# Three instead of two chunk pairs a stage as seven block products, and two of the four weight sums made by adding DMA loads

## Chip, cores and metric

The kernel runs on one core of a Trainium2 chip. The metric is device time in microseconds (us) of one execution; the kernel before has a median of 1264.96 us over 3 runs (1264.08 to 1266.33).

## What is computed

Two layers; each has two feed-forward stages (FFN) with a mixer between them, all in float32 on 256 rows of 1024. Cut to the part that the change touches:

```
def swiglu(h, wi, wo):
    gate, up = jnp.split(h @ wi, 2, axis=-1)
    return (jax.nn.silu(gate) * up) @ wo
...
    for l in range(DEPTH):
        h = rms_norm(x, ffn1_pre_g[l])
        x = x + 0.5 * rms_norm(swiglu(h, ffn1_wi[l], ffn1_wo[l]), ffn1_post_g[l])
        h = rms_norm(x, mix_pre_g[l])
        ...
        h = rms_norm(x, ffn2_pre_g[l])
        x = x + 0.5 * rms_norm(swiglu(h, ffn2_wi[l], ffn2_wo[l]), ffn2_post_g[l])
```

So there are four FFN stages. The first product, `h @ wi`, has 1024 x 5632 weights, the second 2816 x 1024.

## The kernel before

**Tiling.** The 256 rows are two token tiles of 128 (`tt`). The 2816 hidden columns are 11 chunks of 256 gate and 256 up columns, so a chunk of the first product is one 128x512 accumulator per token tile. A unit is 1 MB of weights (128 partitions x 2048); a chunk's first product takes two units (`u11`, `u21` for its lower and upper 512 contraction rows), its second product one. To reach float32 accuracy every weight is split into two parts: ScalarE rounds half a unit to `hi` (line 217), VectorE computes the residue `lo` (line 218), and TensorE makes three matmuls of 512 columns (`mm3`, lines 383 to 385). TensorE takes `hi` and `lo` from a ring of 8 half units, which is 4 units: a slot is free again when TensorE has used it.

**Chunk pairs.** Two neighbouring chunks, two token tiles and two halves of the contraction make 8 block products of 12 matmuls each. For the pairs that begin at a chunk in `QUADS`, `pair7` makes them from 7 products by a Strassen-like scheme. Its weight operands are seven units, in the order of the plan: `B11` (u11), `T2`, `B21` (u21), `T3`, `T1`, `T4`, `B22` (u22), with two units `w` of the second product between them: B11, T2, w, B21, T3, T1, w, T4 (its weights are sum `f`), B22. Four of the operands are sums: T1 = u11 + u12, T2 = u11 + u12 + u22, T3 = u12 + u22, T4 = T2's sum + u21. They are made in tiles `a` (u11, later T1; `wa` in the profile), `b` (u12, later T3; `wb`) and `f` (T2, later T4; `wf`).

**Order of the work.** A planner with estimated times (`Clock`) writes every engine's instruction list at build time; on the chip each engine works through its list in order. The generator `loader` issues the loads on SP's queue, a few items ahead of `splitter`, which issues `hi`, `lo` and the sums. Plain units stream through two buffers of 1 MB (`raw`). Loads of `a` and `b` for one pair wait until T1 of the pair before has been split, since `a` still holds its weights.

**Accumulators of the first product** rotate through two buffers (`pmm`, tag "mm"). A pair takes four in turn: b0, b1, then a third for T1's product, to which B22's is added, and a fourth for T4. What frees the third is a subtraction on VectorE (`post`, line 536) that starts once B22's product is complete:

```
            b0 = mm()
            prod(b0, *s1, take(1)[0], True)
            chunk(j + 1, 1, b0, u3, ALU.subtract)
            wo2(j - 1)
            b1 = mm()
            prod(b1, *A(1, 4), take(1)[0], True)
            chunk(j, 1, b1, u3, ALU.add)
            prod(b0, *s4, take(1)[0], False)
            chunk(j + 1, 0, b0, u2, ALU.subtract)
```

In the kernel before, the pair at chunk 4 and the pair at chunk 8 each are followed by two units of the second product, which use other accumulators; chunks 6 and 7 are plain.

Of the kernel before, what the change touches and what calls it, by code (L numbers as in the profile page):

```python
# [13 lines left out]
ALU = mybir.AluOpType  # L14
# [10 lines left out]
EPS = 1e-6  # L25
NEG = -1.0e30
UNITS = 106
QUADS = (4, 8)

NOSYNC = mybir.DependencyInfo(mybir.DependencyClass.NoSync, mybir.DependencyReason.DATA)  # L30
HOT = 60
# [4 lines left out]
def f32(ap):  # L36
    return ap.bitcast(F32)
# [40 lines left out]
def trunk(ctx, tc, x, wpk, gains, lnp, wst, bst, consts, out, depth=DEPTH):  # L78
    nc = tc.nc
    V, S, G, T = nc.vector, nc.scalar, nc.gpsimd, nc.tensor  # L80
# [11 lines left out]
    def nm(s):  # L92
        cnt[0] += 1
        return f"{s}_{cnt[0]}"
# [18 lines left out]
    def load(dst, src):  # L113

        i = nc.sync.dma_start(dst, src)
        if lastdma[0] is not None:
            tc.add_manual_dep(i.ins, lastdma[0].ins.name, NOSYNC, reason="load order")
        lastdma[0] = i
# [9 lines left out]
    for l in range(depth):  # L128
        for st0, qj in ((0, QUADS), (33, None), (73, QUADS)):
            b = UNITS * l + st0  # L130
# [4 lines left out]
            def c(j, q):  # L135
                return b + (2 * j if j < 2 else 3 * j - 1 if j < NCH - 1 else 28) + q
# [5 lines left out]
            for j in range(2, NCH - 1, 2):  # L142
                if j in qj:
                    k = Quad({}, c(j, 0), c(j, 1), c(j + 1, 0), c(j + 1, 1))
# [12 lines left out]
    WQ = (slice(0, 1024), slice(1024, 2048))  # L157
    done, raw = set(), {}

    def loader():  # L160

        ring = []

        def stream(key, u, first=False):
            while len(ring) >= 2 and ring[-2] not in done:
                yield
            ring.append(key)
            t = rp.tile([P, 2048], F32, tag="raw", name=f"raw{u}", bufs=2)
            raw[key] = [t[:, c] for c in WQ]
            for c in WQ if first else (slice(0, 2048),):  # L170
                load(t[:, c], wpk[u][:, c])

        for n, (kind, k) in enumerate(plan):
            if kind == "w":
                yield from stream(n, k, n == 0)
            elif kind == "B11":
                while k.prev and not k.prev.t1:
                    yield
                f = k.ffn
                if not f:  # L180
                    for t in "ab":
                        f[t] = [sp.tile([P, 1024], F32, tag="q4", name=nm("w" + t), bufs=9) for _ in WQ]
                raw[n] = f["a"]
                for t, u in ((f["a"], k.u11), (f["b"], k.u12)):
                    for q, c in enumerate(WQ):
                        load(t[q], wpk[u][:, c])
                yield from stream(k, k.u22)
            elif kind in ("B21", "B22"):
                yield from stream(n, k.u21 if kind == "B21" else k.u22)
            yield  # L190

    ld = loader()

    def ready(n, kind, k):
        if kind[0] == "T":
            raw[n] = k.ffn[{"T1": "a", "T2": "f", "T3": "b", "T4": "f"}[kind]]
        return n in raw and (kind != "B11" or k in raw)

    def splitter():
        for n, (kind, k) in enumerate(plan):  # L200
            while not ready(n, kind, k):
                next(ld)
            halves[n] = []
            for q in range(2):
                gate = place.get(n)
                while st_["free"] <= 0 if gate is None else not gate.on:
                    yield 0.2
                    gate = place.get(n)
                if gate is not None:
                    h = sp.tile([P, 1024], F32R, tag="q4", name=f"hi{n}_{q}", bufs=9)  # L210
                    lo = sp.tile([P, 1024], F32R, tag="q4", name=f"lo{n}_{q}", bufs=9)
                else:
                    st_["free"] -= 1
                    h = rp.tile([P, 1024], F32R, tag="hi", name=f"hi{n}_{q}", bufs=RING)
                    lo = rp.tile([P, 1024], F32R, tag="lo", name=f"lo{n}_{q}", bufs=RING)
                r = raw[n][q]
                S.copy(h, r)  # L217
                V.tensor_sub(lo, r, f32(h))  # L218
                halves[n].append((h, lo))
                yield 1.2  # L220
            if kind == "B11":
                f = k.ffn
                if "f" not in f:
                    f["f"] = [sp.tile([P, 1024], F32, tag="xn", name=nm("wf"), bufs=2) for _ in WQ]
                for q in range(2):
                    V.tensor_add(f["a"][q], f["a"][q], f["b"][q])
                    V.tensor_add(f["f"][q], f["a"][q], raw[k][q])
                    yield 1.2
            elif kind == "T2":
                for q in range(2):  # L230
                    V.tensor_add(k.ffn["b"][q], k.ffn["b"][q], raw[k][q])
                    yield 0.6
                done.add(k)
            elif kind == "B21":
                for q in range(2):
                    V.tensor_add(k.ffn["f"][q], k.ffn["f"][q], raw[n][q])
                    yield 0.6
            elif kind == "T1":
                k.t1 = True
            done.add(n)  # L240
            for _ in range(3):
                next(ld, None)
# [27 lines left out]
    def gain(i):  # L270
        if i not in gl and i < 6 * depth:
            t = sp.tile([P, DM], F32, tag="gain", name=f"gain{i}", bufs=2)
            load(t, gains[i:i + 1, :].broadcast_to([P, DM]))
            gl[i] = t
        return gl.get(i)
# [149 lines left out]
    def ffn(gi, nxt, first):  # L425
# [3 lines left out]
        always.on = True  # L429
        for i in (32 + 3 * len(QUADS), 33 + 3 * len(QUADS)):  # L430
            place[st_["pos"] + i] = always
# [143 lines left out]
        for j in range(2, NCH - 1):  # L575
            if j == 4:
# [3 lines left out]
                gain(gi + 2)  # L580
            if j // 2 * 2 in QUADS:
                if j % 2 == 0:
# [333 lines left out]


    ck.start(splitter(), 7.0)
    for tt in range(NT):
        hready[tt] = Flag()  # L920
# [5 lines left out]
    for l in range(depth):  # L926
        b = 6 * l
# [102 lines left out]
```

## Time and profile before

| | us |
|---|---|
| median of 3 runs | 1264.96 |
| the profiled execution, its own time | 1265.89 |
| its span, first to last instruction | 1263.5 |
| TensorE busy in the span | 1248.7 (99%) |
| VectorE busy | 930.6 (74%) |
| ScalarE busy | 701.8 (56%) |
| GpSimd (POOL) busy | 34.6 (3%) |

Matmuls overlap, so a busy TensorE is to be read with the distance from one matmul's start to the next. The DMA engines moved 242.62 MB. About 0.2% (2.5 us) is what a measurement of this kernel can tell from no change.

### The profile page before, as it was taken

The numbers are of one execution on the slowest core, as the hardware profiler recorded it, in microseconds if no ns is written. First come the engines' busy times: TensorE is split into PE (matmuls) and PEld (weight loads), VectorE is DVE, ScalarE is ACT, GpSimd is POOL, SyncE is SP. The second block draws the span as 40 slices with busy tenths as digits, with TensorE's granted clock in tenths as the row PEclk, the third lists the DMA queues.
The fourth block names the chain that finished last, engine by engine and source line by source line (L and its number), as shares of the span: only waits on it lengthen the run. The fifth ranks groups of instructions, "written<-read, shape, count | busy, mean of one in ns | idle before, by whom it ended". The sixth has DMA issues, their size and how long they took to land.

```text
span 1263.5 us, 16239 instructions
## 1 busy us (share of the span) xinstructions
PE 1248.7 (99%) x6332; PEld 1040.4 (82%) x6332; DVE 930.6 (74%) x1157; ACT 701.8 (56%) x968; POOL 34.6 (3%) x81
## 2 busy tenths in 40 slices
PE   8999999999999999999999999999999999999997
PEld 7788888998778888888888888789977788888886
DVE  5897977646765979878768878765466568798783
ACT  6565665445666555656655646644366655556462
POOL 0000001000000010000000000010000000000000
PEclk9999999999999999999999999999999999999999
DMA  7757465555335545675645665654544355465651
GB/s 250 267 196 294 141 235 178 195 182 192 112 131 200 199 167 200 215 252 170 215 175 197 213 252 192 220 190 163 204 168 134 134 197 200 143 227 208 223 189 63
DMA packets 38381, 242.62 MB, mean 192 GB/s; under 512 B 4512, under 2 KB 4640, under 8 KB 12320
## 3 DMA queue, kind: packets, MB, share of 16 engines
q1 hardware_dynamic: 38304, 241.59, 54.1%
q8 instruction: 49, 0.80, 0.2%
q14 instruction: 28, 0.23, 0.1%
HBM read 240.52 MB, written 1.05 MB: 191 GB/s over the span
## 4 chain that ended last, share of the span: by engine, by line
PE 91%; DVE 4%; DMA 2%; ACT 2%; issue 1%; POOL 0%; SPq 0%; DVEq 0%; POOLq 0%; ACTq 0%
PE mm L383 16%; PE mm L385 16%; PE mm L384 16%; PE acc L385 6%; PE acc L384 6%; PE acc L383 6%; PE qk L384 3%; PE qk L383 3%; PE qk L385 3%; PE tr L330 3%; DMA raw<-wpk 2%; DVE lo L218 2%; PE pj L385 1%; PE pj L383 1%; PE pj L384 1%; ACT hi L217 1%
## 5 line engine op out<-in xcount | busy, mean ns | idle before, releaser
L218 DVE TENSOR_TENSOR lo<-raw,hi 128x1024 fp32r<-128x1024 f32 x392 | 470.2, 1221 | 166.2 <-ACT hi L217 160.8
L217 ACT CAST hi<-raw 128x1024 fp32r<-128x1024 f32 x392 | 402.9, 1049 | 266.2 <-DMA raw<-wpk 72.4
L383 PE MATMUL mm<-hi,hh 128*128 128x512 f32 x864 | 344.8, 399 | 1.1 <-ACT hh L323 1.1
L385 PE MATMUL mm<-hi,hl 128*128 128x512 f32 x864 | 338.4, 392 | 0.2 <-DVE hl L324 0.2
L384 PE MATMUL mm<-lo,hh 128*128 128x512 f32 x864 | 338.3, 392 | 0.0
L383 PEld LDWEIGHTS mm<-hi,hh 128*128 128x128 f32 x864 | 162.8, 188 | 36.0 <-issue 2.7
L385 PEld LDWEIGHTS mm<-hi,hl 128*128 128x128 f32 x864 | 162.6, 188 | 35.5 <-DVE hl L324 0.9
L384 PEld LDWEIGHTS mm<-lo,hh 128*128 128x128 f32 x864 | 163.1, 189 | 30.9
L383 PE MATMUL acc<-hi,gT 128*128 128x512 f32 x352 | 140.5, 399 | 0.0
L385 PE MATMUL acc<-hi,gT 128*128 128x512 f32 x352 | 138.0, 392 | 0.0
L384 PE MATMUL acc<-lo,gT 128*128 128x512 f32 x352 | 137.5, 390 | 0.0
L383 PE MATMUL qk<-hh,hi 128*128 128x256 f32 x320 | 91.3, 285 | 0.0
L385 PE MATMUL qk<-hh,lo 128*128 128x256 f32 x320 | 90.7, 284 | 0.0
L384 PE MATMUL qk<-hl,hi 128*128 128x256 f32 x320 | 90.7, 284 | 0.0
L385 PEld LDWEIGHTS acc<-hi,gT 128*128 128x128 f32 x352 | 66.1, 188 | 13.9
L384 PEld LDWEIGHTS acc<-lo,gT 128*128 128x128 f32 x352 | 66.3, 188 | 12.7
L383 PEld LDWEIGHTS acc<-hi,gT 128*128 128x128 f32 x352 | 66.2, 188 | 12.7 <-ACT gT L323 0.2
L323 ACT CAST gT<-tr 128x256 fp32r<-128x256 f32 x88 | 32.5, 369 | 73.8 <-PE tr L330 73.6
L384 PEld LDWEIGHTS qk<-hl,hi 128*128 128x128 f32 x320 | 61.5, 192 | 0.1
L383 PEld LDWEIGHTS qk<-hh,hi 128*128 128x128 f32 x320 | 61.5, 192 | 0.1
L385 PEld LDWEIGHTS qk<-hh,lo 128*128 128x128 f32 x320 | 61.5, 192 | 0.0
L324 DVE TENSOR_TENSOR gT<-tr,gT 128x256 fp32r<-128x256 f32 x88 | 36.8, 419 | 20.8 <-ACT gT L323 20.1
(170 smaller groups left out, 1552.3 us busy)
## 6 DMA issues: line engine op xcount, KB each, us to landing
raw<-wpk SPq DMA_DIRECT2D x203, 1024.0 KB, 4.9
wa<-wpk SPq DMA_DIRECT2D x16, 512.0 KB, 7.0
wb<-wpk SPq DMA_DIRECT2D x16, 512.0 KB, 8.9
gain<-gains SPq DMA_DIRECT2D x12, 512.0 KB, 7.1
x<-x SPq DMA_DIRECT2D x2, 512.0 KB, 5.6
raw<-wpk SPq DMA_DIRECT2D x2, 512.0 KB, 6.5
ln<-lnp SPq DMA_DIRECT2D x4, 256.0 KB, 5.7
out<-x SPq DMA_DIRECT2D x4, 256.0 KB, 2.0
```

The source lines that it names most:

```text
L217: S.copy(h, r)
L218: V.tensor_sub(lo, r, f32(h))
L323: lasthi[0] = S.copy(h_out, src)
L324: V.tensor_sub(l_out, src, f32(h_out))
L330: T.transpose(tr[:, k * P:(k + 1) * P], src[:, k * P:(k + 1) * P], ident)
L383: T.matmul(o, ah, bh, start=first, stop=False, skip_group_check=go_on)
L384: T.matmul(o, ah, bl, start=False, stop=False, skip_group_check=go_on)
L385: T.matmul(o, al, bh, start=False, stop=stop, skip_group_check=go_on)
```

## The change

Chunks 6 and 7 become a pair as well, so that a stage has three pairs in a row (chunks 4 to 9). In all pairs, two sums move from VectorE to DMA: T3 = b + u22 and T1 = a + u12 are made by DMA loads issued from GpSimd's queue that add what they read to what lies in the tile. The loads of u22 and u12 for this come to 2 MB a pair; before, u22 was loaded once for it into a `raw` buffer, and u12 was not loaded a second time. T2's sum is now f = a + b, after b has become u12 + u22, and before a becomes u11 + u12.

```
-QUADS = (4, 8)
+QUADS = (4, 6, 8)
...
                 for t, u in ((f["a"], k.u11), (f["b"], k.u12)):
                     for q, c in enumerate(WQ):
                         load(t[q], wpk[u][:, c])
-                yield from stream(k, k.u22)
+                for q, c in enumerate(WQ):
+                    nc.gpsimd.dma_start(f["b"][q], wpk[k.u22][:, c], accum_op=ALU.add)
...
-        return n in raw and (kind != "B11" or k in raw)
+        return n in raw
...
-                for q in range(2):
-                    V.tensor_add(f["a"][q], f["a"][q], f["b"][q])
-                    V.tensor_add(f["f"][q], f["a"][q], raw[k][q])
-                    yield 1.2
-            elif kind == "T2":
-                for q in range(2):
-                    V.tensor_add(k.ffn["b"][q], k.ffn["b"][q], raw[k][q])
+                for q, c in enumerate(WQ):
+                    V.tensor_add(f["f"][q], f["a"][q], f["b"][q])
+                    nc.gpsimd.dma_start(f["a"][q], wpk[k.u12][:, c], accum_op=ALU.add)
                     yield 0.6
-                done.add(k)
```

How it moves instructions, at three places of the second FFN stage of layer 0. TensorE's list of the kernel before, where the pair at chunk 4 ends (`mm_4535` is its third accumulator, B22's product the last written to it; `acc` are accumulators of the second product):

```order
L385 MATMUL mm_4535<-hi_1_4544,sA_4217 128x512
L383 MATMUL acc_4111<-hi_0_4556,gT_4511 128x512 [waits Activation_49]
L384 MATMUL acc_4111<-lo_0_4557,gT_4511 128x512
L385 MATMUL acc_4111<-hi_0_4556,gT_4511 128x512
L330 MATMUL tr_4661<-ident,cc_4630 128x128 [waits DVE_49,PE_49]
```

The same place in the changed kernel (`mm_4562` is the third accumulator, `mm_4686` the next pair's first, and of the same buffer):

```order
L381 MATMUL mm_4562<-hi_1_4571,sA_4242 128x512
L379 MATMUL mm_4686<-hi_0_4583,hh 128x512 [waits DVE_49,Activation_49]
L380 MATMUL mm_4686<-lo_0_4584,hh 128x512
L381 MATMUL mm_4686<-hi_0_4583,hl 128x512
L379 MATMUL mm_4686<-hi_0_4583,hh 128x512
```

The second product's matmuls no longer stand between the pairs: B11's product of the next pair comes straight behind, and its first matmul waits for VectorE.

VectorE's list of the kernel before, from the first pair's B11 to the residues of T2, with the eight adds of `a`, `b` and `f` (six of them here):

```order
L218 TENSOR_TENSOR lo_1_4275<-wa_4136,hi_1_4274 128x1024 [waits DMAHW1_49,Activation_49]
L226 TENSOR_TENSOR wa_4135<-wa_4135,wb_4137 128x1024 [waits DMAHW2_49,DVE_49]
L324 TENSOR_TENSOR gT_4220<-tr_4294,gT_4220 128x256 [waits Activation_49]
L227 TENSOR_TENSOR wf_4284<-wa_4135,raw_4194 128x1024 [waits DMAHW4_49,DVE_49]
L226 TENSOR_TENSOR wa_4136<-wa_4136,wb_4138 128x1024 [waits DMAHW3_49]
L231 TENSOR_TENSOR wb_4137<-wb_4137,raw_4194 128x1024
L227 TENSOR_TENSOR wf_4285<-wa_4136,raw_4194 128x1024 [waits DVE_49]
L218 TENSOR_TENSOR lo_0_4308<-wf_4284,hi_0_4307 128x1024 [waits Activation_49]
L231 TENSOR_TENSOR wb_4138<-wb_4138,raw_4194 128x1024
L218 TENSOR_TENSOR lo_1_4319<-wf_4285,hi_1_4318 128x1024 [waits Activation_49]
```

VectorE's list of the changed kernel from B11 of the pair at chunk 6 to the subtraction that frees `mm_4562` (DMASW is a DMA issued by GpSimd; `raw_4528` is the unit `w` behind T2):

```order
L219 TENSOR_TENSOR lo_1_4599<-wa_4159,hi_1_4598 128x1024 [waits DMAHW3_49]
L227 TENSOR_TENSOR wf_4309<-wa_4158,wb_4160 128x1024 [waits DMASW0_49]
L320 TENSOR_TENSOR gT_4592<-tr_4618,gT_4592 128x256 [waits Activation_49]
L227 TENSOR_TENSOR wf_4310<-wa_4159,wb_4161 128x1024 [waits DMASW1_49]
L219 TENSOR_TENSOR lo_0_4630<-wf_4309,hi_0_4629 128x1024 [waits Activation_49]
L219 TENSOR_TENSOR lo_1_4641<-wf_4310,hi_1_4640 128x1024 [waits Activation_49]
L219 TENSOR_TENSOR lo_0_4651<-raw_4528,hi_0_4650 128x1024 [waits DMAHW6_49,Activation_49]
L532 TENSOR_TENSOR cc_4657<-mm_4636,u_4420 128x512 [waits PE_49]
L219 TENSOR_TENSOR lo_1_4665<-raw_4528,hi_1_4664 128x1024 [waits Activation_49]
L532 TENSOR_TENSOR cc_4683<-mm_4562,u_4420 128x512 [waits PE_49]
```

Two adds stand where six stood, each waits for an adding load, and the subtraction stands behind them and behind five residues.

GpSimd's list of the changed kernel, where the stage begins (before, this queue held no DMA):

```order
L312 TENSOR_TENSOR rs_3997<-rs_3997,mh 128x1 [waits Pool_49]
L188 DMA wb_4160<-wpk 128x1024 [waits DMASW4_49,DMAHW2_49,DVE_49,PE_49]
L188 DMA wb_4161<-wpk 128x1024 [waits DMASW5_49,DMAHW3_49,DVE_49,PE_49]
L228 DMA wa_4158<-wpk 128x1024 [waits DMASW6_49,DMASW2_49,DMAHW0_49,DVE_49,Activation_49]
L228 DMA wa_4159<-wpk 128x1024 [waits DMASW7_49,DMAHW1_49,DVE_49,Activation_49]
L188 DMA wb_4160<-wpk 128x1024 [waits DMAHW4_49,DMASW0_49]
```

Twelve adding DMAs a stage stand between the norms' small operations, and those of `b` wait for SP's loads of `b` (DMAHW).

## Rows read from the trace of the kernel before

**Rows 1.** The page's first part: span, busy time of each engine.

```profile
span 1263.5 us, 16239 instructions
PE 1248.7 (99%) x6332; PEld 1040.4 (82%) x6332; DVE 930.6 (74%) x1157; ACT 701.8 (56%) x968; POOL 34.6 (3%) x81
```

**Rows 2.** Busy time by stretch: layer 0's second FFN stage, its first pair.

```profile
core 0: us, PE busy (x) PEld busy (x) DVE busy (x) ACT busy (x) POOL busy (x), PEclk, DMA share, GB/s
450.00:624.00 174.00, 174.00 (x795) 143.41 (x794) 142.90 (x169) 99.49 (x139) 3.27 (x6) 1.00 0.60 208
...
512.00:542.00 30.00, 30.00 (x137) 24.77 (x136) 26.47 (x31) 20.37 (x25) 0.00 (x0) 1.00 0.63 219
```

**Rows 3.** Timeline of TensorE in that pair: start, duration, operation.

```profile
511.21 0.39 PE L383 MATMUL mm<-hi,hh 128*128 128x512 f32 x1
...
513.93 0.39 PE L383 MATMUL mm<-hi,sA 128*128 128x512 f32 x1
...
527.78 0.39 PE L383 MATMUL mm<-hi,sA 128*128 128x512 f32 x1
...
541.65 0.39 PE L385 MATMUL mm<-hi,sA 128*128 128x512 f32 x1
541.88 0.39 PE L383 MATMUL acc<-hi,gT 128*128 128x512 f32 x1
```

**Rows 4.** Timeline of VectorE in that pair.

```profile
501.23 1.22 DVE L231 TENSOR_TENSOR wb<-wb,raw 128x1024 f32<-128x1024 f32 x1
502.37 1.22 DVE L227 TENSOR_TENSOR wf<-wa,raw 128x1024 f32<-128x1024 f32 x1
...
519.63 2.36 DVE L218 TENSOR_TENSOR lo<-wa,hi 128x1024 fp32r<-128x1024 f32 x2
...
540.18 1.23 DVE L218 TENSOR_TENSOR lo<-raw,hi 128x1024 fp32r<-128x1024 f32 x1
541.32 0.42 DVE L470 TENSOR_TENSOR cc<-cc 128x256 f32<-128x256 f32 x1
541.65 1.22 DVE L218 TENSOR_TENSOR lo<-raw,hi 128x1024 fp32r<-128x1024 f32 x1
542.79 0.68 DVE L536 TENSOR_TENSOR cc<-mm,u 128x512 f32<-128x512 f32 x1
543.39 0.42 DVE L324 TENSOR_TENSOR gT<-tr,gT 128x256 fp32r<-128x256 f32 x1
```

**Rows 5.** The page's costliest groups, ScalarE's rounding: busy, mean ns.

```profile
L217 ACT CAST hi<-raw 128x1024 fp32r<-128x1024 f32 x392 | 402.9, 1049 | 266.2 <-DMA raw<-wpk 72.4
```

**Rows 6.** The chain that ended last, where TensorE waits for VectorE: start, duration.

```profile
191.01 0.34 DVE sg L443
191.36 0.04 issue
191.40 0.44 PE tr L330 x2
```

**Rows 7.** The page's DMA issues: KB each, median us to landing; SP's timeline.

```profile
raw<-wpk SPq DMA_DIRECT2D x203, 1024.0 KB, 4.9
wb<-wpk SPq DMA_DIRECT2D x16, 512.0 KB, 8.9
out<-x SPq DMA_DIRECT2D x4, 256.0 KB, 2.0
...
548.33 0.90 SPq L115 DMA_DIRECT2D wa<-wpk  x2
549.27 1.15 SPq L115 DMA_DIRECT2D wb<-wpk  x2
```

**Rows 8.** Timeline of GpSimd, and of VectorE beside its second row.

```profile
804.58 0.30 POOL L313 TENSOR_SCALAR rs<-ss 128x1 f32<-128x1 f32 x1 [161.60 <-ACT sq L363]
...
820.91 1.05 POOL L313 TENSOR_SCALAR rs<-ss 128x1 f32<-128x1 f32 x1 [12.00 <-ACT sq L363]
...
820.58 1.22 DVE L218 TENSOR_TENSOR lo<-raw,hi 128x1024 fp32r<-128x1024 f32 x1
```

## The prediction

> **What bounds the kernel now.** I read the busy times first, then the stretches, then the lists of TensorE and VectorE in one pair, row by row. TensorE is busy for 1248.7 of 1263.5 us [rows 1]; in the second FFN stage of layer 0 for 174.00 of 174.00, with VectorE at 142.90 and the DMA engines at a share of 0.60 [rows 2]. So the stage is as long as its matmuls, and what counts is how many of them there are and whether TensorE ever has to stop. I take this stage for all four. A product of 12 matmuls takes 513.93 - 511.21 = 2.72 us, a whole pair with its two `w` units 541.88 - 511.21 = 30.67 us [rows 3]. VectorE's instructions overlap a little: from one start to the next a residue or an add takes 1.14 us (540.18 to 541.32, 501.23 to 502.37), a subtraction 0.60 (542.79 to 543.39), a small operation 0.33 [rows 4].
>
> How far VectorE is ahead is what the change eats into. Before, the first residue of T1 is ready at 519.63 + 1.22 = 520.85, and TensorE wants it at 527.78: a lead of 6.9 us [rows 3, 4].
>
> **What it removes.** One product a stage: 4 x 2.72 = 10.9 us of TensorE, at full value since TensorE does not wait there. On VectorE a pair loses four adds (4.6 us), which buys lead, not time. T1's slot in the ring is that of T2, whose first half is used by 513.93 + 1.36 = 515.3; rounding (1.05 [rows 5]) and residue (1.22) end at 517.6 at the earliest. I take T1 ready at 518.0 in the first pair, a lead of 9.8 us.
>
> **What it adds, first: a stop between neighbouring pairs.** Before, the last matmul of B22 starts at 541.65 and the next matmul, on another accumulator, at 541.88; the subtraction that empties B22's accumulator starts only at 542.79 [rows 3, 4]. Nobody waits for it. After, B11's product of the next pair goes into that very buffer, and there are two such places a stage (4 to 6, 6 to 8), eight in all. The least price: the last matmul ends 0.39 after its start, VectorE starts about 0.04 later and takes 0.68, and TensorE starts 0.04 after that (the 0.04 is the "issue" piece between VectorE and TensorE [rows 6]): 1.15 us after the last matmul's start instead of 0.23, a stop of 0.92 us; I use 1.0, so 8.0 for the eight. Nothing hides it: TensorE's list has nothing else there.
>
> **Second: the stop is longer when VectorE is late,** because in its list the subtraction stands behind the adds of f, T2's residues and those of the next `w`. I count from t0, the end of T1's first residue. To the end of the last residue ahead of the subtraction there are 13 residues and 2 adds at 1.14, 3 subtractions at 0.60 and 4 small ones at 0.33: 20.3 us. TensorE, if not stopped, ends the pair 541.88 - 527.78 = 14.1 us after it takes up T1, that is lead + 14.1 after t0. Behind the stop: from that last residue to the end of T1's first residue of the next pair VectorE has 7 of 1.14, 2 of 0.60, 4 of 0.33: 10.5 us. TensorE restarts 0.64 after the residue and takes up T1 16.6 later (527.78 - 511.21). So the second place starts with a lead of 0.64 + 16.6 - 10.5 = 6.7 us whatever the first cost. A period of VectorE is 30.8 us against TensorE's 30.67: it has no room left to catch up.
>
> **Third: the wait for the adding loads.** The add f = a + b stands 12.5 us of VectorE's work behind t0. It needs the loads of a and b, which wait for T1's residues (1.14 more for the second half), and then the adding loads, which wait for b. After that residue a's second half (0.45) and b's first (0.6) are issued, so b's second goes out at t0 + 2.2, and it lands 8.9 us after issue in the median [rows 7]: b is complete at t0 + 11.1. From there to the adding load's landing, X, no row exists. Both halves are 1 MB from HBM. Lower bound: a plain 1 MB lands in 4.9; upper: a half of b, queued behind others, in 8.9 [rows 7]. A 256 KB store lands in 2.0, so X could be below the lower row if the two halves overlap with b's own landing; I keep that for a rival. I take X = 6.0, nearer the lower end, because the DMA share of the pair is 0.63 [rows 2] and the 2 MB of adding loads stand against 1 MB of u22 that goes away, but above it since the next `w` and B21 load at the same time and the sum has to be read as well as written. So both halves of f can start at a = 11.1 + 6.0 = 17.1 after t0. From a to the last residue there are the add (1.2), T2's two residues, `w`'s two and one subtraction: 1.2 + 4 x 1.14 + 0.60 = 6.4 us. Subtraction and restart add 0.64: TensorE restarts at a + 7.0. Behind the waiting add stand, on VectorE, those residues and the subtractions that empty the accumulators, and TensorE waits for them; on ScalarE, T2's rounding waits as well, with `w`'s behind it.
>
> Stop at the first place: a + 7.0 - (9.8 + 14.1) = a - 16.9, but at least 1.0. At the second: a + 7.0 - (6.7 + 14.1) = a - 13.8, but at least 1.0. With a = 17.1: 1.0 and 3.3, 4.3 us a stage, 17.2 in all. **Sum:** 17.2 - 10.9 = +6.3 us. Against the profiled execution's own 1265.9 that is 1272.2; this execution lies 0.9 above the median of the runs, so I say 1271. With X = 4.9 (a = 16.0): 1.0 + 2.2, sum +1.9, 1267. With X = 8.9 (a = 20.0): 3.1 + 6.2, sum +26.3, 1291.
>
> **A rule on X.** GpSimd's small operation that takes 0.30 us alone took 1.05 at 820.91, and ended 0.16 after the residue begun at 820.58 [rows 8]. If each adding load's issue waited for a residue in this way, the two of b would add up to 2.4 us: a = 19.5, stops 2.6 + 5.7, sum +22. [...] No row here shows a DMA issued by GpSimd.
>
> [...]
>
> **Costed at nothing.** ScalarE's 6 more roundings for the new pair: it is busy 20.37 of 30 us in a pair [rows 2]; were it late, VectorE would be late by as much. T1's adding load: it starts after f, with T2, `w`, two adds, B21 and T3 (ten instructions of 1.14, some 11 us) before T1's rounding needs it; a load slower than that makes T1 late by the rest. GpSimd's queue: the norms' operations stand behind the stage's twelve DMAs, and these are over long before the stage ends. The second load of u12: 4 MB a stage with the new pair's u22, in a queue that is idle 0.40 of the time.
>
> **Rivals.**
> *Adding loads that land at once* (the other side). If a is 14.8 or less, X below 3.7, both stops fall to 1.0: 8.0 - 10.9 = -2.9, 1262. For it speaks the 2.0 us store; against it the 4.9 of a plain MB. The turning point for faster at all is a = 15.5 (sum 0).
> *Slow adding loads* (X near 8.9 or held up by VectorE): the periods of VectorE stretch to 33 us and more and the second place pays most: 1285 to 1295. For it the 1.05 of GpSimd's operation [rows 8] and the queues that already make b land in 8.9.
> *The stop does not come*, because the wait in TensorE's list is met before it matters: then the whole 10.9 comes, 1254. I see no reason for it: the buffer is the same.
>
> **How the numbers follow.** Forecast, X between 4.9 and 7.5, 1266 to 1280: 0.45. Loads that land at once, 1261 to 1266: 0.22. Slow loads, 1280 to 1300: 0.25. No stop: 0.05. Anything else: 0.03. The range 1261 to 1293 leaves out the whole gain and the slowest of the slow. 0.2% is 2.5 us, about what a measurement can tell from no change: faster (below 1262.4) is half of the second case and the fourth, 0.16; same is its other half and the lower part of the first, 0.23; slower 0.61.
>
> **What the profile after should show.** TensorE with 4 x 12 = 48 fewer matmuls of the first product; eight gaps of 1 to 4 us in its list ahead of `mm<-hi,hh`, released by `cc`, the second of a stage longer than the first; VectorE idle ahead of `wf<-wa,wb`, released by a DMA, for up to 5 us in the pairs at 6 and 8; adding loads of 5 to 8 us to landing. I am wrong if the gaps are all 1 us (loads faster than thought), if they lie elsewhere (T1 late for its own adding load, plain loads starved), or if VectorE's adds do not wait and the time still rises.

## The result: 67 us slower, 40 us beyond the end of the range

The changed kernel takes 1332.55 us (median of 4 runs, 1329.12 to 1343.11) against 1265.18 for the kernel before beside it: a ratio of 1.0546 (95% interval 1.0487 to 1.0606). The forecast was 1271, and the range ended at 1293. The profiled execution took 1332.06 us.

The page of the changed kernel (parts 1, 3, 5 and 6; the columns of part 3 are packets, MB, and the share of 16 engines' span), for [rows 1], [rows 5] and [rows 7]:

```profile
span 1330.4 us, 16365 instructions
PE 1261.6 (95%) x6284; PEld 1043.0 (78%) x6284; DVE 951.4 (72%) x1185; ACT 728.8 (55%) x996; POOL 76.1 (6%) x129
...
q1 hardware_dynamic: 38304, 233.20, 49.7%
q0 software_dynamic: 6912, 25.17, 10.7%
...
L218 ACT CAST hi<-wf 128x1024 fp32r<-128x1024 f32 x48 | 50.3, 1049 | 93.1 <-DVE wf L227 78.4
...
L227 DVE TENSOR_TENSOR wf<-wa,wb 128x1024 f32<-128x1024 f32 x24 | 29.4, 1225 | 73.0 <-DMA wb<-wpk 73.0
...
wb<-wpk SPq DMA_DIRECT2D x24, 512.0 KB, 8.6
wb<-wpk POOLq DMA_DIRECT2D x24, 512.0 KB, 9.8
wa<-wpk POOLq DMA_DIRECT2D x24, 512.0 KB, 5.8
```

The matmuls are 6284 in place of 6332, the 48 fewer that the change promised. The add of f waits 73.0 us for b's adding load, which lands 9.8 us after its issue in the median; ScalarE's rounding of f waits 78.4 us behind that add.

Stretches of layer 0's second FFN stage: from T1 of the pair at 4 to T1 of the pair at 6, from there to T1 of the pair at 8, and 5.5 us behind a stop, for [rows 2]:

```profile
core 0: us, PE busy (x) PEld busy (x) DVE busy (x) ACT busy (x) POOL busy (x), PEclk, DMA share, GB/s
541.00:579.00 38.00, 35.12 (x153) 28.48 (x152) 31.16 (x37) 22.85 (x29) 3.44 (x4) 0.96 0.84 242
579.00:620.00 41.00, 34.78 (x146) 27.88 (x145) 31.61 (x36) 21.47 (x27) 3.45 (x4) 0.92 0.72 202
...
608.36:613.90 5.54, 5.54 (x14) 4.14 (x15) 5.17 (x8) 3.90 (x6) 0.00 (x0) 0.51 0.75 192
```

A pair takes 38 to 41 us where TensorE has work for 30.67. VectorE works 31.2 to 31.6 of it and waits for the rest. Where TensorE stopped, it goes on at a granted clock of 0.51 (the last row, 5.54 us); over the whole span it is 0.974, and 0.999 in the kernel before.

TensorE's timeline at the two places between pairs, for [rows 3]: the last matmul of B22, and the first ones of the next pair's B11.

```profile
566.05 0.39 PE L381 MATMUL mm<-hi,sA 128*128 128x512 f32 x1
569.32 0.69 PE L379 MATMUL mm<-hi,hh 128*128 128x512 f32 x1 [2.88 <-DVE cc L532]
...
601.75 0.39 PE L381 MATMUL mm<-hi,sA 128*128 128x512 f32 x1
608.36 0.77 PE L379 MATMUL mm<-hi,hh 128*128 128x512 f32 x1 [6.22 <-ACT hi L218]
```

VectorE's timeline there, for [rows 4]:

```profile
542.17 2.35 DVE L219 TENSOR_TENSOR lo<-wa,hi 128x1024 fp32r<-128x1024 f32 x2
...
563.78 1.23 DVE L227 TENSOR_TENSOR wf<-wa,wb 128x1024 f32<-128x1024 f32 x1 [3.17 <-DMA wb<-wpk]
564.92 2.51 DVE L219 TENSOR_TENSOR lo<-wf,hi 128x1024 fp32r<-128x1024 f32 x2
...
568.49 0.69 DVE L532 TENSOR_TENSOR cc<-mm,u 128x512 f32<-128x512 f32 x1
...
570.22 0.69 DVE L532 TENSOR_TENSOR cc<-mm,u 128x512 f32<-128x512 f32 x1
...
580.35 2.35 DVE L219 TENSOR_TENSOR lo<-wa,hi 128x1024 fp32r<-128x1024 f32 x2
...
601.51 1.23 DVE L227 TENSOR_TENSOR wf<-wa,wb 128x1024 f32<-128x1024 f32 x1 [6.98 <-DMA wb<-wpk]
...
603.98 1.23 DVE L227 TENSOR_TENSOR wf<-wa,wb 128x1024 f32<-128x1024 f32 x1 [0.91 <-DMA wb<-wpk]
...
607.53 0.68 DVE L532 TENSOR_TENSOR cc<-mm,u 128x512 f32<-128x512 f32 x1
...
610.74 0.68 DVE L532 TENSOR_TENSOR cc<-mm,u 128x512 f32<-128x512 f32 x1
```

TensorE goes on 0.14 and 0.15 us after the end of the first of two instructions of VectorE that empty accumulators (569.18 and 608.21). That one is `post` for T4's product, an addition in the code. The second, the subtraction that empties B22's accumulator, starts only after TensorE has gone on (570.22, 610.74). So the next pair's first accumulator is the one that T4's product leaves, and not the third, B22's, as the section on the change has it; TensorE waited for T4's addition. At 608.36 the profile names ScalarE's rounding, which ends at 608.26; the same 0.15 speaks for the addition. Either way it stands behind the add of f.

The chain that ended last, in order of time, from T1 of the pair at 6 to the second restart, for [rows 6]:

```profile
579.22 3.50 DVE lo L219 x3
582.73 0.33 SPq L115
583.15 8.70 DMA wb<-wpk
591.89 0.49 issue
592.38 0.76 POOL wb L188
593.14 0.47 issue
593.63 10.32 DMA wb<-wpk
603.98 1.24 DVE wf L227
605.46 0.81 issue
606.27 2.00 ACT hi L218 x2
608.26 0.10 issue
608.36 0.77 PE mm L379
```

I read this as the loop that sets the pace: T1's residues free a, the loads of a and b go out, the last of them lands after 8.7 us, GpSimd issues two adding loads 1.25 us apart, the second lands after 10.3, and only then f goes on. None of it is TensorE's. At the first place (569.32) the chain names a matmul of TensorE ahead of ScalarE's rounding of f's second half at 565.12. But that rounding starts 0.11 us after the end of the add of f (563.78 + 1.23 = 565.01), as the roundings at 560.39 and 605.31 start 0.11 and 0.10 after theirs, so I take it for the same wait.

### The profile page after: what moved, and what is told of

The parts are those of the page before. It is cut to its first block, busy times and chain, and to the rows that moved or that the text cites. A ratio compares the mean times of both kernels' runs of the same rounds, so it can differ in the third digit from the quotient of the medians.

```text
span 1330.4 us, 16365 instructions
## 1 busy us (share of the span) xinstructions
PE 1261.6 (95%) x6284; PEld 1043.0 (78%) x6284; DVE 951.4 (72%) x1185; ACT 728.8 (55%) x996; POOL 76.1 (6%) x129
## 3 DMA queue, kind: packets, MB, share of 16 engines
q1 hardware_dynamic: 38304, 233.20, 49.7%
q0 software_dynamic: 6912, 25.17, 10.7%
HBM read 257.30 MB, written 1.05 MB: 194 GB/s over the span
## 4 chain that ended last, share of the span: by engine, by line
PE 62%; DMA 20%; DVE 8%; ACT 4%; issue 3%; POOL 1%; SPq 1%; POOLq 0%; ACTq 0%; DVEq 0%
DMA wb<-wpk 16%; PE mm L379 11%; PE mm L381 10%; PE mm L380 10%; DVE lo L219 4%; DMA raw<-wpk 4%; PE qk L379 3%; PE qk L380 3%; PE qk L381 3%; ACT hi L218 3%; PE acc L381 3%; PE acc L380 3%; PE acc L379 3%; PE tr L326 2%; PE pj L379 1%
## 5 line engine op out<-in xcount | busy, mean ns | idle before, releaser
L219 DVE TENSOR_TENSOR lo<-raw,hi 128x1024 fp32r<-128x1024 f32 x376 | 451.4, 1219 | 148.8 <-ACT hi L218 144.2
L218 ACT CAST hi<-raw 128x1024 fp32r<-128x1024 f32 x376 | 386.6, 1049 | 257.8 <-DMA raw<-wpk 66.3
L379 PE MATMUL mm<-hi,hh 128*128 128x512 f32 x784 | 322.0, 411 | 45.9 <-ACT hi L218 31.5
L380 PE MATMUL mm<-lo,hh 128*128 128x512 f32 x784 | 314.1, 401 | 0.0
L381 PE MATMUL mm<-hi,hl 128*128 128x512 f32 x784 | 313.4, 400 | 0.2 <-DVE hl L320 0.2
L381 PEld LDWEIGHTS mm<-hi,hl 128*128 128x128 f32 x784 | 151.7, 194 | 34.1 <-DVE hl L320 0.9
L218 ACT CAST hi<-wf 128x1024 fp32r<-128x1024 f32 x48 | 50.3, 1049 | 93.1 <-DVE wf L227 78.4
L227 DVE TENSOR_TENSOR wf<-wa,wb 128x1024 f32<-128x1024 f32 x24 | 29.4, 1225 | 73.0 <-DMA wb<-wpk 73.0
L379 PE MATMUL mm<-hi,sA 128*128 128x512 f32 x192 | 77.3, 402 | 0.0
L381 PE MATMUL mm<-hi,sA 128*128 128x512 f32 x192 | 75.2, 392 | 0.0
L380 PE MATMUL mm<-lo,sA 128*128 128x512 f32 x192 | 74.9, 390 | 0.0
```

What stands on the lines that cost most here:

```text
L227: V.tensor_add(f["f"][q], f["a"][q], f["b"][q])
L379: T.matmul(o, ah, bh, start=first, stop=False, skip_group_check=go_on)
L380: T.matmul(o, ah, bl, start=False, stop=False, skip_group_check=go_on)
L381: T.matmul(o, al, bh, start=False, stop=stop, skip_group_check=go_on)
```

## The experiments

Each was timed in 4 to 11 runs beside the kernel before (1265.5 to 1265.9 us).

**1. Two pairs a stage, sums by adding loads** (second part of the change alone).

```diff
-QUADS = (4, 6, 8)
+QUADS = (4, 8)
```

> Two pairs a stage as before (chunks 4 and 8), but with both adding loads: the second part of the change alone. Theory A (b's adding load lands about 10 us after its issue, VectorE waits for it in the add of f, and TensorE stops): the stops that the changed kernel shows in the first pair of a stage (5.1, 1.8 and 2.1 us in three of the four) stay, and one like them may come in the pair at 8, which now has a lead again from the plain chunks ahead of it: 1270 to 1290, slower than before. Theory B (three pairs in a row are what VectorE and the loads can't keep up with, whatever makes the sums): no stops, and VectorE has fewer adds: 1262 to 1267.

1303.77 us, ratio 1.0299 (1.0261 to 1.0337). Slower than A's upper end, and far from B. The add of f waits 54.7 us for b's adding load, and TensorE's transposes wait 30.9 us (3.6 in the kernel before), up to 4.8 at a time, for an instruction of VectorE behind that add. The adding loads, b's and T1's together, cost 38 us with no third pair at all.

**2. Three pairs, all sums on VectorE** (first part alone).

```diff
-                for q, c in enumerate(WQ):
-                    nc.gpsimd.dma_start(f["b"][q], wpk[k.u22][:, c], accum_op=ALU.add)
+                yield from stream(k, k.u22)
```

The sums are those of the kernel before.

> Three pairs a stage, all sums on VectorE as before, u22 loaded into a raw buffer: the first part of the change alone. Theory A: VectorE's period of a pair is about 35 us against TensorE's 30.7, so it loses some 4 us a pair and its lead of 7 is gone in the third: stops of 0 to 6 us a stage, 1255 to 1280. Theory B: the stops are as many and as long as in the changed kernel, 1300 or more. [...]

1311.03, ratio 1.0352 (1.0333 to 1.037): beyond A's 1280, and as B said. VectorE works 1003.2 us here, 51.8 more than in the changed kernel, and in the stretch of 42 us to T1 of the third pair it is busy for 35.51. So its work is more than TensorE's 30.67 of a pair, but not the whole 42; the other 6.5 us, in which VectorE, ScalarE and TensorE wait for one another, I did not take apart.

**3. T1's sum alone by an adding load**, T3's by VectorE.

```diff
+                    V.tensor_add(f["b"][q], f["b"][q], raw[k][q])
                     V.tensor_add(f["f"][q], f["a"][q], f["b"][q])
                     nc.gpsimd.dma_start(f["a"][q], wpk[k.u12][:, c], accum_op=ALU.add)
```

u22 for b comes by `stream`, as in experiment 2.

> Three pairs a stage; T1's sum by an adding load as in the changed kernel, T3's sum (b = b + u22) by VectorE from a plain load, ahead of f. No add waits for an adding load whose load was issued in the same step. Theory A: the wait for b's adding load is gone, VectorE's period is about 33 us against 30.7, stops of a few us in the third pair at most: 1254 to 1272, possibly faster than before. Theory B: 1300 or more as in the changed kernel. If T1's adding load (issued some 11 us ahead of its use, landing after 6 to 10) is late by itself, TensorE stops at T1 and the time is between the two.

1274.35, ratio 1.0065 (1.005 to 1.008): just above A's range, 58 us less than the changed kernel. So the third pair and T1's adding load, the same as there, are not what costs most. They are not free either: this run is 8.8 us slower than the kernel before, though it has the 48 matmuls less.

**4. The changed kernel without b's adding loads.**

```diff
-                for q, c in enumerate(WQ):
-                    nc.gpsimd.dma_start(f["b"][q], wpk[k.u22][:, c], accum_op=ALU.add)
```

> The changed kernel without the two adding loads of b: u22 is left out of the sums T2 and T3 (part of the computation is left out), everything else stays. f then waits for b's plain load alone, t0 + 11.1 in the terms of the prediction instead of t0 + 20 to 22. Theory A: nearly all stops and the half clock behind them go: 1252 to 1262. Theory B: the stops stay, over 1290. A value between them says how much of the wait is that of the plain loads of a and b, which start only when T1 of the pair before has been split.

The sums T2 and T3 lack u22 here, so part of the computation is left out. 1258.48, ratio 0.9942 (0.9927 to 0.9957), within A's range. f's wait for b is 4.2 us in all. So b's 24 adding loads are worth 74 us, all of the loss and more. Whether it is the wait for them or their traffic, experiment 12 tells.

**5. b's second load plain, not adding.**

```diff
-                    nc.gpsimd.dma_start(f["b"][q], wpk[k.u22][:, c], accum_op=ALU.add)
+                    nc.gpsimd.dma_start(f["b"][q], wpk[k.u22][:, c])
```

> The changed kernel with b's second load made a plain one: same queue (GpSimd's), same bytes, same waits, but u22 overwrites u12 instead of being added to it (T2 and T3 are then other sums). It prices the adding alone. Theory A1 (the adding is what is slow): the second load lands 4 to 6 us after its issue instead of a median of 9.8, f waits some 4 us less, and the time falls to 1265 to 1300. Theory A2 (it is a load that may only start when another has landed, among a stage's other transfers; adding or not does not matter): it still lands after 9 to 10, and the time stays at 1320 to 1335. The run without any second load of b took 1258.5.

1295.06, ratio 1.023 (1.0215 to 1.0246): A1, though near the end of its range. Page parts 3 and 6 and the waits (us in total, times, longest):

```profile
q0 software_dynamic: 6912, 25.17, 8.3%
...
wb<-wpk POOLq DMA_DIRECT2D x24, 512.0 KB, 6.9
```

```profile
DVE wf L227 <- DMA wb<-wpk: 35.5, 10, 5.0
```

The plain load lands after 6.9 us, the adding one after 9.8. So of the 74 us about half (36.6) is that a second load follows a first one, and half (37.5) that it adds. The adding loads of T1, of the same size, land after 5.8 us in the changed kernel: how late a load lands depends on its place as well. What in b's place does it was not separated.

**6. b's loads first, after T3 of the pair before.**

```diff
-                while k.prev and not k.prev.t1:
+                while k.prev and not k.prev.t3:
                     yield
```

The loads of b follow, and behind them the wait for t1 and the loads of a.

> The changed kernel with the loads of b (u12) issued before those of a, as soon as T3 of the pair before has been split and no longer after T1; the adding loads follow as before, some 4 to 5 us earlier in the pairs at 6 and 8. The first pair of a stage gains only the order (about 1 us). Theory A: the stops between pairs (5.9 and 7.4 us, 3.3 and 6.6, 4.9 and 7.1, 5.8 and 6.4 in the four stages) shrink by 4 to 5 each, and much of the half clock behind them goes: 1275 to 1295. Rival (the DMA engines are full in this stretch, a share of 0.89 to 0.93, so earlier transfers only push others back): 1315 to 1335.

1309.69, ratio 1.0345 (1.031 to 1.038), between the two theories. f's wait falls from 73.0 to 48.6 us. The slowest load of `wb` now takes 15.0 us to land (11.7 in the changed kernel), though the medians don't rise (6.7 and 9.7 against 8.6 and 9.8); that the loads of a beside them take back some of the gain is likely but not shown.

**7. The stops filled with matmuls.**

```diff
+        zero = sp.tile([P, 2, 384], F32R, tag="sh", name=nm("zero"), bufs=1)[:, 0, 0:P]
+        V.tensor_scalar(zero, ident, 0.0, None, op0=ALU.mult)
...
+            if j > QUADS[0]:
+                for i in range(22):
+                    T.matmul(acc[0][i % 2], zero, hh[:, 0, 0:4, :], start=False, stop=False, skip_group_check=True)
             prod(b0, *A(0, 0), take(1)[0], True)
```

> The changed kernel with 22 matmuls more on TensorE at each place between neighbouring pairs, ahead of the one that waits; they add zeros to the second product's accumulators, wait for nothing, and take 22 x 0.23 = 5.1 us of what is now a stop of 3.3 to 7.4 us. Theory C (the half clock behind each stop, 17 us of longer pitch in all, is a price of its own that falls with the idle time): TensorE keeps its clock and gets 10 to 17 us back, less about 2 us where a stop was shorter than 5.1: 1315 to 1323. Rival (TensorE at full clock only arrives earlier at the next wait, since VectorE and the loads set the pace): 1328 to 1340.

1332.43, ratio 1.0527 (1.0509 to 1.0544): the rival. TensorE's mean granted clock is 0.988 (0.974 in the changed kernel, 0.999 in the kernel before), and the time is the same. Its timeline at the place of the 6.6 us stop, and the wait of f:

```profile
602.31 5.15 PE L549 MATMUL acc<-hh,zero 128*128 128x512 f32 x22
610.47 0.47 PE L379 MATMUL mm<-hi,hh 128*128 128x512 f32 x1 [3.01 <-DVE cc L534]
...
612.53 0.66 PE L326 MATMUL tr<-ident,cc 128*128 128x128 f32 x2 [1.13 <-DVE cc L468]
612.84 0.78 PE L379 MATMUL mm<-hi,hh 128*128 128x512 f32 x1
```

```profile
DVE wf L227 <- DMA wb<-wpk: 74.7, 23, 7.5
```

The 22 matmuls lie in the stop, and the first product matmul behind it takes 0.47 in place of 0.77. After three of them TensorE waits again, 1.13 us, and from 612.53 to about 615 it is at the slower pace after all (0.78, then 0.63 for a matmul that takes 0.39 at full pace). So about half of the lost clock comes back over the run, and the time doesn't: TensorE's transposes now wait 8.2 us for `cc` of VectorE, 0.9 in the changed kernel. The slower clock behind a stop is a fact of the trace, but giving back that much of it won no time.

**8. T1's and T4's sums by adding loads, T3's on VectorE.** As experiment 3, with

```diff
-                    V.tensor_add(k.ffn["f"][q], k.ffn["f"][q], raw[n][q])
+                    nc.gpsimd.dma_start(k.ffn["f"][q], wpk[k.u21][:, c], accum_op=ALU.add)
```

issued once T2 is split.

> Three pairs a stage, two of the four sums by adding loads again, but the two that have time: T1 (a + u12, some 11 us ahead of its use) and T4 (f + u21, issued once T2 is split, some 15 us ahead); T3 = b + u22 and f = a + b are made by VectorE. VectorE has four adds a pair as in the changed kernel, and no add waits for an adding load. Theory A: stops of 0 to 2 us a stage: 1254 to 1265. Rival (a pair then moves 7 MB plainly and 2 MB by adding loads, whose engine time counts twice, against 6 and 2: the DMA engines fill up): loads come late, 1270 to 1300.

1288.91, ratio 1.0178 (1.0155 to 1.02): the rival's range. That is 14.6 us slower than experiment 3, with two adds a pair less on VectorE. ScalarE's timeline:

```profile
601.32 2.00 ACT L217 CAST hi<-raw 128x1024 fp32r<-128x1024 f32 x2 [6.53 <-DMA raw<-wpk]
```

f's adding loads land after 12.5 us in the median, and ScalarE waits 6.5 us for a plain unit there. The DMA engines are at a share of 0.92 in the stretch before it (567 to 600 us), in which TensorE is still busy for 32.86 of 33.00. That full engines are the cause fits this, but no run separates it.

**9. A fifth tile for b**, so that one adding load and not two stands in the loop.

```diff
+                k.b = [f["b"][0], f["c"][0] if k.prev and k.prev.b[1] is f["b"][1] else f["b"][1]]
...
+                    while q == 0 and k.prev and not k.prev.t3:
+                        yield
+                    load(k.b[q], wpk[k.u12][:, c])
+                    nc.gpsimd.dma_start(k.b[q], wpk[k.u22][:, c], accum_op=ALU.add)
```

> The changed kernel with a fifth tile for b: its second half changes between two tiles from pair to pair, so its load and its adding load need not wait for the pair before; the first half is loaded after T3 of the pair before is split (as in the run with b first), and the loads of a come last. One adding load of 512 KB, no longer two, stands in the loop from T1 of one pair to f of the next. Theory A (the loop of loads, adding loads and VectorE sets the pace: 38 to 42 us a pair in the changed kernel, of which VectorE is busy for 31.4): the loop falls to 32 to 33, 1258 to 1275. Rival F (the DMA engines are full: a pair moves 6 MB plainly and 2 MB by adding loads whose engine time counts twice, by the queues' shares about 29.7 us of every engine): transfers come late elsewhere, 1280 to 1310.

1307.5, ratio 1.0324 (1.0289 to 1.0358): the rival's range. But f's wait for b is still 51.0 us: the adding load now lands after 11.8 in the median, beside the loads of a. So it is again that wait; that the engines are full is not shown by it.

**10. Experiment 3 with T4's sum on GpSimd**, and **11. experiment 2 with T3's and T4's sums on GpSimd.**

```diff
-                    V.tensor_add(k.ffn["f"][q], k.ffn["f"][q], raw[n][q])
+                    G.tensor_add(k.ffn["f"][q], k.ffn["f"][q], raw[n][q])
```

> Three pairs a stage; T1's sum by an adding load and T3's by VectorE as in the run that took 1274.4, and T4's sum (f + u21) moved from VectorE to GpSimd, which has some 15 us for it. That run's loop was as long as VectorE's work in it (33.3 to 33.8 us busy of 34 to 39). Theory A (VectorE's work sets it): two adds less, 2.3 us a pair, eight times: 1255 to 1262, faster than before. Rival G (GpSimd's add waits for VectorE, as its small operations did in the kernel before, 1.05 us for 0.30, or holds VectorE up): T4 late, 1275 or more.

> Three pairs a stage, no adding loads: T1 = a + u12 and f = a + u22 by VectorE as before, T3's and T4's sums by GpSimd (T3 has some 8 us, T4 some 15). VectorE has four adds a pair and the DMA engines only 7 MB of plain loads. Theory A: 1254 to 1262, faster than before. Rival G (GpSimd and VectorE hold each other up): four adds of GpSimd a pair come late, T3 first: 1285 or more, towards the 1311 of the run with all sums on VectorE.

1319.25 (1.0419, 1.0402 to 1.0436) and 1346.03 (1.0646, 1.0604 to 1.0689): G in both. Timelines of GpSimd and of VectorE in experiment 11:

```profile
558.31 2.39 POOL L231 TENSOR_TENSOR wb<-wb,raw 128x1024 f32<-128x1024 f32 x1 [19.87 <-DVE wa L226]
562.99 3.42 POOL L231 TENSOR_TENSOR wb<-wb,raw 128x1024 f32<-128x1024 f32 x1 [2.30 <-DVE wa L226]
572.60 5.58 POOL L236 TENSOR_TENSOR wf<-wf,raw 128x1024 f32<-128x1024 f32 x2 [6.19 <-DMA raw<-wpk]
```

```profile
558.48 3.29 DVE L227 TENSOR_TENSOR wf<-wa,raw 128x1024 f32<-128x1024 f32 x1
564.12 3.38 DVE L227 TENSOR_TENSOR wf<-wa,raw 128x1024 f32<-128x1024 f32 x1
...
573.36 2.58 DVE L470 TENSOR_TENSOR cc<-cc 128x256 f32<-128x256 f32 x1
```

VectorE's add of 1.22 us takes 3.3 beside GpSimd's, and a small one of 0.42 takes 2.58. The adds of VectorE at 558.48 and 564.12 end 1.07 and 1.09 us after GpSimd's (560.70, 566.41). Over the run VectorE is busy for 996.0 us in experiment 10, against 976.2 in 3 with 24 adds more, and for 1040.7 in 11, against 1003.2 in 2 with 48 more. So here, with 19.8 and 37.5 us more on VectorE for 24 and 48 adds fewer, GpSimd's add took more of VectorE's time than the add that it saved.

**12. All loads kept, f without b.**

```diff
-                    V.tensor_add(f["f"][q], f["a"][q], f["b"][q])
+                    V.tensor_add(f["f"][q], f["a"][q], f["a"][q])
```

> The changed kernel with f = a + a in place of a + b (T2 and T4 are then other sums): all loads and adding loads stay, but VectorE's add of f no longer waits for b's adding load; b is first needed by T3's rounding, three units later. Theory A (the wait of f for b's adding load is what costs: 73 us of waiting against 74 us lost to the run without that load): 1258 to 1265. Rival F (it is the traffic of the adding loads, which holds up other loads wherever it is waited for): 1285 or more.

T2 and T4 are other sums here. 1262.68, ratio 0.9978 (0.9967 to 0.9989): A. The adding loads still run, at a median of 9.7 us, and the DMA engines are as full as anywhere:

```profile
517.00:550.00 33.00, 31.98 (x146) 25.98 (x145) 29.32 (x35) 22.22 (x28) 3.43 (x4) 1.00 0.94 279
550.00:583.00 33.00, 33.00 (x151) 27.10 (x150) 32.54 (x38) 21.57 (x27) 3.45 (x4) 1.00 0.88 253
```

TensorE is busy for 64.98 of these 66 us. The traffic costs 4.2 us (1262.68 against the 1258.48 of experiment 4); the wait costs the other 70.

**13. Experiment 3 with b's sums ahead of f's**, and **14. with b's sums ahead of B11's residues too.**

```diff
+                for q in range(2):
+                    V.tensor_add(f["b"][q], f["b"][q], raw[k][q])
+                done.add(k)
+                for _ in range(3):
+                    next(ld, None)
                 for q, c in enumerate(WQ):
-                    V.tensor_add(f["b"][q], f["b"][q], raw[k][q])
                     V.tensor_add(f["f"][q], f["a"][q], f["b"][q])
                     nc.gpsimd.dma_start(f["a"][q], wpk[k.u12][:, c], accum_op=ALU.add)
...
```

`next(ld)` lets the loader go on at once, so the loads move up in their list too.

> The run with T1's sum alone as an adding load (1274.4) with VectorE's list changed: both adds b = b + u22 stand ahead of the two adds of f, so that the buffer of u22 is free one add and one half of f sooner, and u21 (B21's unit, which goes into that buffer) is loaded some 2 us earlier. In that run u21's rounding waited 3.0 us for its load in the first pair of a stage, VectorE idled 1.8 us behind it, and TensorE stopped for 2.2 to 2.5 us where the pair ends. Theory A (VectorE's 33.3 us a pair against 30.7 of TensorE eats the lead of 7 to 10 without a stop; the rest of the 9 us lost is that late load): 1262 to 1270. Rival H (VectorE's work is what costs, the load only shows it): 1272 to 1276.

> As the run before this one, with the two adds of b ahead of B11's residues too, so that u21 is loaded as early as b and u22 have landed; B11's residues and f come later by what VectorE waits for them. Theory A: like that run or 1 to 4 us faster, 1260 to 1269, since TensorE wants B11 only after the pair before has ended. Rival H: 1272 to 1276; if VectorE waits long for u22, which is loaded behind a and b, slower than 1276.

1263.01 (ratio 0.9974, 0.9965 to 0.9983), within A's range, and 1271.19 (1.0044, 1.003 to 1.0058), between A's and H's. Experiment 13 computes everything and beats both kernels, the kernel before by 2.9 us, just over the 2.5 that a measurement can tell. Page part 1 of experiment 3, and then of 13:

```profile
PE 1245.6 (98%) x6284; PEld 1029.4 (81%) x6284; DVE 976.2 (77%) x1209; ACT 723.8 (57%) x996; POOL 53.8 (4%) x105
```

```profile
PE 1242.3 (99%) x6284; PEld 1028.9 (82%) x6284; DVE 976.2 (77%) x1209; ACT 723.8 (57%) x996; POOL 53.6 (4%) x105
```

VectorE and ScalarE work exactly as long; the order, of the adds and of the loads with them, is worth 11.3 us. In experiment 3 u21's rounding waited 3.02 us for its load at 547.28; in 13 that wait is gone, and f's second half is also earlier. Which of the two gives how much is not separated. In 14 VectorE waits up to 4.07 us for u22, with B11's residues and an accumulator's `cc` behind it, and TensorE's first product waits up to 1.8 us for a `cc`.

## Why the prediction failed, step by step

**The steps that failed are the "third", in its term X, and the price of a wait in that loop.** The direction was right, and so was the place: the adds of f in the pairs at 6 and 8, released by a DMA. But I gave X, from b's landing to the landing of the adding loads, 6.0 us with 8.9 as its upper bound. At the second place b lands at 591.89, the first adding load is issued 0.49 later, the second at 593.63, and that lands 10.32 after, at 603.95: X was 12.1. In the prediction's terms a was 563.78 - 543.39 = 20.4 at the first place and 603.98 - 581.57 = 22.4 at the second, against 17.1. The 8.9 was the largest median among the plain loads of the trace; nothing made it a bound for a load of another kind.

With these two values of a the prediction's formula gives stops of 3.5 and 8.6 us, 48.4 in the four stages, and a sum of +37.5. TensorE's waits at the eight places are near that, 44.3 us in all (us in total, times, longest):

```profile
PE mm L379 <- ACT hi L218: 31.5, 5, 7.0
PE mm L379 <- DVE cc L532: 12.8, 3, 5.4
```

So X makes about half (37.5 - 6.3 = 31.2) of the 61 us between forecast and result. The rest is in what the formula doesn't charge: it counts only the stops, and the time followed f's waits. The waits of `wf` for `wb` against the time above experiment 4's (which has the third pair, T1's adding load, and 4.2 us of this wait):

| kernel | f waits for b, us | above 1258.48, us |
|---|---|---|
| 5, plain second load | 35.5 | 36.6 |
| 6, b first | 48.6 | 51.2 |
| 9, fifth tile | 51.0 | 49.0 |
| changed kernel | 73.0 | 74.1 |
| 7, stops filled | 74.7 | 74.0 |

Each us of f's wait came back in the time; less experiment 4's 4.2 us, one of wait goes with 1.05 to 1.17 of time. The prediction let 16.9 and 13.8 us of a pass free. But from T1 of the pair at 6 to f of the next the chain holds nothing of TensorE's, and in a whole pair VectorE is busy for 31.2 to 31.6 us, already more than TensorE's 30.67: an idle 7 us there is made up by nothing. That this is why a wait counts in full is argued from these rows; the five kernels show only that it does.

**Left out: the first pair of a stage.** I asked for its lead and not for its adding loads. In experiment 1, where pairs never follow each other, the kernel with these loads is 38 us slower; in the changed kernel they stop TensorE in the first pair as well, for 4.7, 1.4 and 1.7 us in three of the four stages.

**The "first" step named the wrong buffer.** B11's product goes to the accumulator that T4's addition frees, 4.4 us after the second add of f starts at the second place (603.98 to 608.36) and not 7.0. This erred the other way: with a = 22.4 the formula's stop would have been 8.6; with 4.4 it is 22.4 + 4.4 - 20.8 = 6.0, and the trace has 608.36 - 601.75 - 0.23 = 6.4. The rival "the stop does not come" was set aside because "the buffer is the same". It isn't, but T4's addition stands behind f in VectorE's list too.

**Not foreseen, and nothing to be won by it here: the clock.** TensorE is busy 12.9 us longer than in the kernel before, with 10.9 us less to do: behind the stops its matmuls come every 0.43 instead of 0.23 us. By adding up gaps one can put part of the loss down to that. But experiment 7 gives back about half of the lost clock and gets no time for it.

**"No room left" on VectorE** was too strict for a third pair. Experiment 13 has six adds a pair, 24.8 us more VectorE work than the changed kernel (976.2 against 951.4), and is 69.5 us faster.

**Right:** the 48 matmuls fewer. Of the 10.9 us for them experiment 4 got 7.1 and experiment 12, with all loads, 2.9. Also the place of the wait, with the second of a stage the longer one in all four; T1's adding load near nothing (experiment 4 has it and is 3.8 us short of the whole 10.9); and the DMA volume near nothing (4.2).

**The rule on X.** GpSimd's issues of b's adding loads took 0.86 to 1.06 us each and did not stretch with VectorE's residues (the one at 592.38 took 0.86 beside the residue of 591.84 to 593.06), so the +22 did not come that way. What the adding loads took more of is the DMA engines' time: 10.7% of 1330.4 us for 25.17 MB is 5.66 us per MB, 49.7% for 233.20 MB is 2.84, a factor of 2.0. In experiment 5, with half of q0's bytes plain, 8.3% of 1292.0 us is 107.2, and 12.58 x (5.66 + 2.84) is 106.9. My 6.0 for X was an estimate between the landing times of two kinds of plain loads, 4.9 and 8.9; 12.1 was measured. How much of that is other traffic beside the adding loads stays open: no run here shows one of b without such traffic.

## What to carry to other kernels

An adding load moves a sum off VectorE, but here it put two landings and the issues between them in a row (8.7, 1.7 and 10.3 us at the second place). Give it only a sum whose result is wanted later than that (even then it can cost: T4's, in experiment 8, made the kernel 14.6 us slower than experiment 3), and trace the loop from the buffer's last reader round to it: here an idle us in a loop as long as TensorE's work cost a whole one (1.05 to 1.17). If the trace lacks an operation, don't take rows of other operations as an upper bound on its price. Before moving work to another engine, look at the order of the list: the same work in another order of adds and loads was worth 11.3 us.

## What was unexpected of the hardware

The adding loads took twice the DMA engines' time of the plain ones (5.66 against 2.84 us per MB), and b's, of 512 KB, landed after 9.8 us in the median where a plain one in its place took 6.9. Beside a GpSimd add of 2.4 to 3.4 us, VectorE's add of 1.22 took 3.3 and its small one of 0.42 took 2.58; the two large adds of VectorE ended 1.07 and 1.09 us after GpSimd's, as if one had run after the other. TensorE came out of a stop of 6.6 us (from matmul start to matmul start) at a granted clock of 0.51 for 5.5 us. With 5.15 us of matmuls in that stop and a wait of 3.01 behind them, the first three matmuls took 0.47, 0.39 and 0.40 us, and after another wait of 1.13 it was at the slower pace for some 2.5 us.
